# Lower attention rates beside the two later input projections of a streaming-encoder step

## The chip, the cores and the metric

One core of a Trainium2 chip runs the whole step as one program. The metric is the device time of one execution in microseconds (us). TensorE (PE) multiplies matrices, VectorE (DVE), ScalarE (ACT) and GpSimd (POOL) do the element-wise work, SyncE (SP) issues all of this kernel's DMA transfers. PE's instructions run in the order in which the program writes them; the order on the other engines is set by the framework.

## The reference

One layer of a hybrid encoder for 32 sample frames and 2048 prompt frames of width 1024, all float32:

```
u = rmsnorm(x) @ w_in                      # q, k, v (8 heads x 64) and 512 pooling channels
z = q.k / 8, for keys before the query only
a = sigmoid(z) * product of (1 - sigmoid(z)) over the keys between    # stick-breaking, no softmax
att = rmsnorm(a @ v);  pool = rmsnorm(multi-scale causal pooling of u's last 512 channels)
x = x + [att, pool] @ w_out                # output projection
x = x + (silu(h @ w_gate) * (h @ w_up)) @ w_down,  h = rmsnorm(x)     # d_ff 2816
x = x + (p @ w_ple) * sigmoid(rmsnorm(x) @ w_ple_gate);  y = rmsnorm(x)
```

The sample frames also see 256 cached keys. The new k, v and pooling rows are outputs too.

## The kernel before, in words

Every large product is done with three matmuls (`mm3`, lines 206 to 208) on operands split into a high and a low part. The 2080 frames go through two kinds of dense stages. Three **projection stages** (`project`, called P0, P1, P2 here) each take two column blocks of `WB` (288 and 384, 384 and 384, 384 and 256 frames) and store q, k, v to DRAM scratch. Then three **later stages** (`rest`, called R0, R1, R2 here) each take two column blocks of `OB` (336 and 336, then 352 each) through output projection, FFN and gated embedding.

**Attention** (`all_units`, `attn_units`, `attention`) is cut into query groups 0 to 6: group 0 is the sample frames, group 1 has 2 query tiles of 128, groups 2 to 5 have 3, group 6 has 2. For each of 8 heads a group has one unit per key segment: its own ("diagonal") segment first, then the earlier groups' segments. A unit with m query tiles and n key tiles has a cost of m*n, a diagonal one m(m+1)/2, one of group 0 a cost of 4 (`TS_COST`). It is handed out in max(m, n) **steps**, each of which writes, in PE's order, one scores product `z` (line 711), for an earlier unit the two `av` products (753, 754), and the transposes `tp` (740) that `av` needs two steps later. Behind `z` come two sigmoids on ACT (714, 715), for diagonal tiles a POOL mask (719), a scan and a product on DVE (729, 730), and behind the transposes the split of `aa` (175 on ACT, 176 on DVE). `z` and `av` have one PSUM bank each. The loads of the next unit's `q`, `kt`, `vt` are issued at the first step of the unit before it. After groups 0 and 1 the pipeline is drained with steps of cost 1. After the last unit of a group come its norm (`norm0` to `norm3`): by `LAGE` the last of it, `norm3`, which stores the group's columns of HX and sets `astate["done"]`, stands about ten steps behind the last unit, so inside the next group for groups 2 and up.

**Who runs when** is set by `drive` (lines 844 to 859): the dense generator yields costs (6 x columns / 2400 for every two of a gemm's k chunks); each is multiplied by the stage's entry in `RATES` and added to a credit, and attention steps are run until the credit is used up. P0 has rate 0; P1 and P2 have `RATES[0]` and `RATES[1]`; R0, R1, R2 have the other three. A group may not start before its q and k exist: groups 0 to 2 in P1, 3 and 4 in P2, 5 and 6 in R0.

```
            att["credit"] += cost * rate
            while att["gen"] is not None and att["credit"] > 0 and att["next"][0] <= ready:
                att["credit"] -= att["next"][1]
                step()
```

**What a later stage needs** stands in `rest` ahead of its first product (line 936): with `NEED = (2, 4, 6)` it runs steps, with nothing between them, until the norm of group 2 (R0), 4 (R1) or 6 (R2) has been written out. Only then come `load_mix`, which loads the attention and pooling columns (`as<-hx`), and, for R0, a yield of 8.0 (`BUBBLE`) ahead of the first output projection.

```
        while att["gen"] is not None and astate["done"] < NEED[OS.index(sup)]:
            step()
```

Of the kernel before, what the change touches and what calls it, by code (L numbers as in the profile page):

```python
# [55 lines left out]
LAGE = (1, 3, 6, 6, 6, 6, 6)  # L56
PREP_LEAD, PREP_COST = 3, 0.5
ACT_SLOTS, X_SLOTS = 26, 20
RATES = (1.1, 1.2, 0.9, 0.9, 0.9)


def MANUAL(nc):
# [16 lines left out]
def stickbreak_step(  # L79
# [764 lines left out]
    def drive(dense, rate, ready):  # L844
        att["ready"] = ready
        for cost in dense:
# [4 lines that stand above are left out]
            if att["credit"] > 0:  # L851
                att["credit"] = 0.0
            bg_n[0] += 1
            if bg and bg_n[0] % BG_EVERY == 0:
                try:
                    next(bg[0])
                except StopIteration:
                    bg.popleft()
# [332 lines left out]
    with tc.manual_schedule(engines=MANUAL(nc)):  # L1191
        with tc.tile_pool(name="proj", bufs=1) as pool, tc.tile_pool(name="projx", bufs=1) as xpool:
            opened = {0: open_block_pair(WS[0], xpool, pool)}

            def following(i):
                if i < len(WS):
                    opened[i] = open_block_pair(WS[i], xpool, pool)
                return opened.get(i)

            for i, sup in enumerate(WS):  # L1200
                drive(project(sup, pool, opened[i], lambda: following(i + 1)), RATES[i - 1] if i else 0.0, i - 1)
        phase["rest"] = True
        with tc.tile_pool(name="rest", bufs=1, reuse_waits="tile") as apool,                 tc.tile_pool(name="restx", bufs=1, reuse_waits="tile") as pool:
            for i, sup in enumerate(OS):
                drive(rest(sup, pool, apool), RATES[2 + i], 2)

# [31 lines left out]
```

## Time and profile before

| | |
|---|---|
| median of 3 runs | 2902.8 us (2901.12 to 2907.18) |
| profiled execution | 2903.48 us |
| its span, first to last instruction | 2901.8 us |
| PE / DVE / ACT / POOL busy | 2828.5 / 2026.4 / 1302.4 / 632.0 us |
| granted PE clock, mean | 0.992 of full speed |
| attention's first and last `z` | 176.5 and 2049.5 us |
| DMA moved | 366.50 MB, mean 126 GB/s |

A matmul's recorded duration overlaps the next one's, so a busy PE is not the measure: a stream of 384-column matmuls has starts about 0.17 us apart while each lasts 0.34 us. What counts is where PE has nothing to start.

### The profile page before, as it was taken

To read this page: it belongs to the slowest core of one execution; us is meant where nothing else is said; L and a number is where in the kernel's file an instruction comes from. 1 tells how busy PE (TensorE), PEld (TensorE's weight loads), DVE (VectorE), ACT (ScalarE), POOL (GpSimd) and SP (SyncE) were. 2 spreads that over 40 slices of the span, in tenths; PEclk is the share of its full clock that TensorE was granted. 3 is DMA by queue.
4 is the path that set the end of the run, shared out by engine and by line. 5 is a ranking of instruction groups with operands and counts; after the bars stand their busy time and mean duration, and the time that the engine had idled before them with its cause. 6 is when DMAs were issued, how large, how long until landed. Compare 5 with 4: busy or idle time off the path is not lost.

```text
span 2901.8 us, 50173 instructions
## 1 busy us (share of the span) xinstructions
PE 2828.5 (97%) x18478; PEld 2783.1 (96%) x18478; DVE 2026.4 (70%) x3498; ACT 1302.4 (45%) x2829; POOL 632.0 (22%) x1175
## 2 busy tenths in 40 slices
PE   7999889999999999999999999999999999999998
PEld 7989789999999999999999999999999999999998
DVE  6466699887878787887888777777555644444466
ACT  4454566655444445455554444444343422222243
POOL 2012223223322222232331221112132210111120
PEclk9999999999999999999999999999999999999999
DMA  6775766783333333323653333333225522222223
GB/s 192 207 226 163 196 192 199 215 257 108 102 114 94 95 92 96 113 88 104 195 175 87 93 118 109 97 102 100 80 80 170 165 73 66 72 67 68 71 86 124
DMA packets 521919, 366.50 MB, mean 126 GB/s; under 512 B 62653, under 2 KB 508925, under 8 KB 521674
## 3 DMA queue, kind: packets, MB, share of 16 engines
q1 hardware_dynamic: 521674, 363.30, 42.3%
q8 instruction: 146, 2.39, 0.3%
q14 instruction: 99, 0.81, 0.1%
HBM read 292.89 MB, written 70.32 MB: 125 GB/s over the span
## 4 chain that ended last, share of the span: by engine, by line
PE 77%; DVE 10%; issue 5%; DMA 3%; ACT 3%; POOL 1%; SPq 0%; DVEq 0%; POOLq 0%; ACTq 0%
PE mm L206 22%; PE mm L207 21%; PE mm L208 21%; PE z L711 4%; PE tp L740 3%; DVE keep L729 2%; PE av L754 2%; PE av L753 2%; DVE wlo L191 2%; DVE as L900 1%; DVE beta L730 1%; DVE aa L176 1%; DVE win L417 1%; ACT whi L190 1%; ACT as L899 1%
## 5 line engine op out<-in xcount | busy, mean ns | idle before, releaser
L206 PE MATMUL mm<-as,whi 128*128 128x352 f32 (+1 forms) x3936 | 1300.3, 330 | 1.6 <-DMA as<-hx 1.6
L207 PE MATMUL mm<-as,whi 128*128 128x352 f32 (+1 forms) x3936 | 1264.8, 321 | 0.0
L208 PE MATMUL mm<-as,wlo 128*128 128x352 f32 (+1 forms) x3936 | 1260.0, 320 | 0.0
L206 PEld LDWEIGHTS mm<-as,whi 128*128 128x128 f32 x3936 | 741.4, 188 | 3.9 <-DMA as<-hx 2.9
L207 PEld LDWEIGHTS mm<-as,whi 128*128 128x128 f32 x3936 | 741.5, 188 | 0.3 <-DVE as L900 0.3
L208 PEld LDWEIGHTS mm<-as,wlo 128*128 128x128 f32 x3936 | 741.6, 188 | 0.0
L190 ACT CAST whi<-wraw 128x1024 fp32r<-128x1024 f32 x326 | 342.5, 1051 | 480.7 <-PE mm L207 457.3
L191 DVE TENSOR_TENSOR wlo<-wraw,whi 128x1024 fp32r<-128x1024 f32 x323 | 395.6, 1225 | 78.1 <-ACT whi L190 77.0
L729 DVE TENSOR_TENSOR_SCAN keep<-keep,keep,zeros 128x384 f32<-128x384 f32 (+2 forms) x328 | 316.6, 965 | 112.0 <-ACT keep L714 111.2
L714 ACT ACTIVATE keep<-z 128x384 f32<-128x384 f32 (+3 forms) x464 | 195.8, 422 | 363.7 <-PE z L711 313.7
L984 POOL TENSOR_TENSOR sg<-sg,t 128x352 f32<-128x352 f32 (+1 forms) x132 | 158.1, 1197 | 729.0 <-ACT sg L959 718.1
L730 DVE TENSOR_TENSOR beta<-beta,keep 128x384 f32<-128x384 f32 (+3 forms) x464 | 236.9, 511 | 31.0 <-POOL beta L719 0.8
L726 POOL COPY keep<-keep 128x1 f32<-128x1 f32 (+1 forms) x328 | 147.9, 451 | 439.7 <-DVE keep L729 438.0
L711 PE MATMUL z<-kt,q 128*128 128x384 f32 (+4 forms) x928 | 212.0, 309 | 17.2 <-ACT beta L715 10.2
L176 DVE TENSOR_TENSOR aa<-tp,aa 128x384 fp32r<-128x384 f32 (+4 forms) x472 | 213.1, 451 | 16.5 <-ACT aa L175 15.7
L175 ACT CAST aa<-tp 128x384 fp32r<-128x384 f32 (+4 forms) x472 | 193.1, 409 | 66.8 <-PE tp L740 60.5
L957 DVE TENSOR_TENSOR t<-mm,rbc 128x352 f32<-128x352 f32 (+1 forms) x180 | 92.8, 515 | 162.9 <-PE mm L208 157.6
L1005 DVE TENSOR_TENSOR xs<-xs,mm 128x352 f32<-128x352 f32 (+1 forms) x288 | 144.2, 509 | 86.2 <-PE mm L208 85.6
L206 PE MATMUL mm<-hh,whi 128*128 128x384 f32 (+2 forms) x576 | 200.0, 347 | 3.8 <-ACT acc L447 2.5
L740 PE MATMUL tp<-ident,beta 128*128 128x128 f32 (+1 forms) x1112 | 199.8, 274 | 0.4 <-ACT xt L331 0.2
L715 ACT ACTIVATE beta<-z 128x384 f32<-128x384 f32 (+3 forms) x464 | 194.4, 419 | 0.0
L208 PE MATMUL mm<-hh,wlo 128*128 128x384 f32 (+2 forms) x576 | 187.4, 325 | 1.0 <-DVE wlo L191 1.0
(155 smaller groups left out, 3748.2 us busy)
## 6 DMA issues: line engine op xcount, KB each, us to landing
wraw<-in_w_ffn_gate_dram SPq DMA_DIRECT2D x66, 512.0 KB, 3.9
wraw<-in_w_ffn_up_dram SPq DMA_DIRECT2D x66, 512.0 KB, 3.9
wraw<-in_w_ffn_down_dram SPq DMA_DIRECT2D x66, 512.0 KB, 3.4
wraw<-in_w_in_dram SPq DMA_DIRECT2D x48, 512.0 KB, 5.0
wraw<-in_w_out_dram SPq DMA_DIRECT2D x48, 512.0 KB, 5.4
kt<-ks SPq DMA_DIRECT2D x112, 192.0 KB, 2.4
vt<-vs SPq DMA_DIRECT2D x112, 192.0 KB, 2.7
wraw<-in_w_ple_gate_dram SPq DMA_DIRECT2D x32, 512.0 KB, 3.9
```

The lines of the kernel that those rows point to most:

```text
L176: V.tensor_sub(lo, src, hi.bitcast(F32))
L190: S.copy(hi, raw)
L191: eng.tensor_sub(lo, raw, hi.bitcast(F32))
L206: T.matmul(ps, a[0], b[0], start=first, stop=False)
L207: T.matmul(ps, a[0], b[1], start=False, stop=False)
L208: T.matmul(ps, a[1], b[0], start=False, stop=last)
L711: T.matmul(z[:qw, :wi], hd["q"][:, e, qsl], un["k"][:, :wi], start=(e == 0), stop=(e == 1))
L714: S.activation(keep[:qw, :wi], z[:qw, :wi], AF.Sigmoid, scale=-0.125)
L715: S.activation(beta[:qw, :wi], z[:qw, :wi], AF.Sigmoid, scale=0.125)
L729: V.tensor_tensor_scan(rev, rev, zeros[:qw].broadcast_to([qw, wi]), initial=init, op0=ALU.mult, op1=ALU.add)
L730: V.tensor_mul(beta[:qw, :wi], beta[:qw, :wi], keep[:qw, 1:wi + 1])
L740: T.transpose(bank[:kw, qo[i]:qo[i] + qws[i]], un["b"][i][:qws[i], k0:k0 + kw], ident[:qws[i], :qws[i]])
```

## The change

Two numbers of one constant: the rates of P1 and P2 go from 1.1 and 1.2 to 0.75 each. The rates of R0 to R2, `NEED` and everything else stay. No instruction is added or taken away; attention steps stand at other places in PE's order, and with them their work on the other engines and their loads.

```diff
-RATES = (1.1, 1.2, 0.9, 0.9, 0.9)
+RATES = (0.75, 0.75, 0.9, 0.9, 0.9)
```

## Rows read from the trace of the kernel before

**Rows 1.** The page: PE's busy time and its share of the span in 40 slices.

```profile
PE 2828.5 (97%) x18478; PEld 2783.1 (96%) x18478; DVE 2026.4 (70%) x3498; ACT 1302.4 (45%) x2829; POOL 632.0 (22%) x1175
...
PE   7999889999999999999999999999999999999998
```

**Rows 2.** Busy time by stretch: P1 (161 to 355), P2 (355 to 573.5), R0 after its start, and the part of R1 that has attention. Columns: stretch, its length, busy time and instructions of PE, PEld, DVE, ACT, POOL, granted PE clock, DMA share, GB/s.

```profile
161.00:355.00 194.00, 176.84 (x1155) 166.23 (x1153) 124.19 (x280) 100.07 (x270) 40.21 (x119) 0.98 0.65 189
355.00:573.50 218.50, 206.77 (x1458) 199.86 (x1458) 194.48 (x374) 139.79 (x354) 68.37 (x163) 0.99 0.69 201
...
587.40:1416.00 828.60, 819.27 (x5416) 808.28 (x5415) 668.77 (x1107) 414.87 (x919) 223.68 (x415) 0.99 0.40 116
1416.00:2066.00 650.00, 647.31 (x4257) 642.11 (x4256) 514.90 (x874) 310.81 (x698) 143.80 (x270) 1.00 0.38 113
```

**Rows 3.** Waits of PE in P1 and P2 (160 to 573.5): who waited, for whom, us in total, times, longest.

```profile
PE z L711 <- DMA kt<-ks: 6.8, 4, 3.6
PE av L753 <- DVE attT L652: 5.0, 6, 1.8
PE tp L325 <- ACT xt L331: 3.4, 3, 1.4
PE z L711 <- ACT beta L715: 3.3, 5, 1.8
PE tp L325 <- DVE xt L333: 3.0, 4, 1.1
PE mm L206 <- ACT acc L447: 2.5, 2, 1.9
PE av L753 <- ACT aa L175: 0.8, 1, 0.8
```

**Rows 4.** Timeline of PE: the column sums of the norm (`norm1`) of group 1, at the end of P1, and of group 2, in P2, and the broadcast (`norm2`) of group 2.

```profile
345.86 0.61 PE L247 MATMUL tp<-ones,aacc 128*128 128x1 f32 x4 [0.16 <-POOL aacc L663]
...
522.26 0.73 PE L247 MATMUL tp<-ones,aacc 128*128 128x1 f32 x6
...
532.05 0.83 PE L268 MATMUL tp<-ident,r 128*128 128x128 f32 x6
```

**Rows 5.** Timeline of PE at the start of R0, where four attention steps stand with no dense product between them (`BUBBLE`): the first product of each step, then the first output projection.

```profile
573.51 0.52 PE L711 MATMUL z<-kt,q 128*128 128x384 f32 x2
...
575.46 0.50 PE L711 MATMUL z<-kt,q 128*128 128x256 f32 x2 [1.22 <-ACT beta L715]
...
577.05 0.51 PE L711 MATMUL z<-kt,q 128*128 128x256 f32 x2 [0.62 <-ACT beta L715]
...
578.55 0.78 PE L711 MATMUL z<-kt,q 128*128 128x256 f32 x2
...
581.23 0.65 PE L206 MATMUL mm<-as,whi 128*128 128x336 f32 x1 [0.77 <-DMA as<-hx]
...
585.48 0.56 PE L206 MATMUL mm<-as,whi 128*128 128x336 f32 x1
```

**Rows 6.** Busy time by stretch around the same place; columns as in rows 2.

```profile
573.50:577.00 3.50, 1.71 (x11) 1.14 (x9) 3.47 (x7) 3.04 (x8) 0.00 (x0) 1.00 0.87 254
577.00:580.40 3.40, 3.34 (x14) 2.73 (x14) 3.40 (x9) 1.95 (x6) 0.73 (x4) 0.58 0.83 262
580.40:587.40 7.00, 5.40 (x17) 4.32 (x17) 2.10 (x5) 0.92 (x3) 0.19 (x2) 0.50 1.06 371
```

**Rows 7.** Timeline of PE in P2: one attention step between dense products, and the dense products behind it.

```profile
558.00 0.33 PE L711 MATMUL z<-kt,q 128*128 128x128 f32 x2
...
558.82 0.43 PE L206 MATMUL mm<-hh,whi 128*128 128x384 f32 x1
559.08 0.34 PE L207 MATMUL mm<-hl,whi 128*128 128x384 f32 x1
559.26 0.34 PE L208 MATMUL mm<-hh,wlo 128*128 128x384 f32 x1
```

**Rows 8.** Groups of DVE instructions from 400 to 573.5, shapes apart: line, engine, operation, tiles, shape, count, then busy us, mean ns of one, then idle time before them.

```profile
L729 DVE TENSOR_TENSOR_SCAN keep<-keep,keep,zeros 128x256 f32<-128x256 f32 x23 | 17.1, 743 | 2.7 <-ACT keep L714 2.7
L176 DVE TENSOR_TENSOR aa<-tp,aa 128x384 fp32r<-128x384 f32 x30 | 16.2, 542 | 0.0
L730 DVE TENSOR_TENSOR beta<-beta,keep 128x256 f32<-128x256 f32 x32 | 14.2, 443 | 1.4
L729 DVE TENSOR_TENSOR_SCAN keep<-keep,keep,zeros 128x384 f32<-128x384 f32 x8 | 8.8, 1103 | 1.0 <-ACT keep L714 1.0
...
L730 DVE TENSOR_TENSOR beta<-beta,keep 128x384 f32<-128x384 f32 x15 | 8.3, 551 | 0.7
...
L652 DVE TENSOR_TENSOR attT<-av,bot 64x384 f32<-64x384 f32 x9 | 4.9, 546 | 0.2
```

**Rows 9.** Timeline of SP at the end of group 2's norm in P2: the issues of the four HX stores (`norm3`).

```profile
536.81 4.00 SPq L95 DMA_DIRECT2D hx<-aa  x3
...
542.77 0.36 SPq L95 DMA_DIRECT2D hx<-aa  x1
```

**Rows 10.** The view of DMA issues: such a store, and a load of R0's columns: engine, operation, count, KB each, median us from issue to landing.

```profile
hx<-aa SPq DMA_DIRECT2D x16, 384.0 KB, 2.7
...
as<-hx SPq DMA_DIRECT2D x16, 336.0 KB, 6.9
```

**Rows 11.** Waits of PE from 587.4 to 2235 (R0 after its start, and R1), the longest.

```profile
PE z L711 <- ACT beta L715: 5.0, 5, 1.5
```

## Prediction

> **What bounds the kernel now.** I read the page first: PE is busy nearly everywhere, and its thin slices are the first seven and a little behind, so whatever a schedule can save lies before about 600 us [rows 1]. Then the stretches: PE lacks 17.2 us of 194.0 in P1 and 11.7 us of 218.5 in P2, while R0 behind its start lacks 9 of 829 and R1 with attention 3 of 650, though both carry attention too [rows 2]. DVE is at 89% in P2 and about 80% in R0 and R1. The granted clock of 0.98 and 0.99 in P1 and P2 stands for some 4 and 2 us more. So at most 17.2 + 11.7 + 6 = 35 us can be had in the two stages that the change thins. Third, whom PE waits for there: for the loads of keys 6.8, for the `av` bank until the head is read out 5.0, for the sigmoids in the single `z` bank 3.3, for the split of `aa` 0.8, together 15.9 us that belong to attention; for x's transposes and for the pooling 3.4 + 3.0 + 2.5 us, which belong to the dense work [rows 3]. In R0 and R1 the longest sort of wait that attention causes is 5.0 us in all [rows 11]. So a step of attention is cheaper beside the later stages, and the direction of the change has a reason in the trace.
>
> **The credit account.** Which steps go where follows from the code alone. Dense costs: P1 yields 16 x 0.5 for the two columns with preparation, 3 x 7.68 for the other pooling columns, 12 x 2.56 for v, 8 x 7.68 for k and q, 123.2; P2 likewise 8 + 3 x 6.4 + 10 x 2.56 + 8 x 6.4 = 104.0. Before, that buys 1.1 x 123.2 + 1.2 x 104.0 = 260 credits. R0 wants group 2's norm written: group 0 costs 16 units x 4 + 11 of drain = 75, group 1 8 x 3 + 11 = 35, group 2 8 x (6 + 6) = 96, and `norm3` stands 11 steps (25 credits: a diagonal unit 6, one on group 2 of 9, one on group 1 of 6, two thirds of a diagonal one 4) into group 3. That is 231, so 260 are enough and the loop of line 936 has nothing to do. The trace agrees: group 2's norm is in P2 at 522 to 532 us, and group 1's at the end of P1 [rows 4].
>
> After, the two stages buy 0.75 x 227.2 = 170, with the overshoot of the last step 172. **The rates fall below what the first output projection needs**: 231 - 172 = 59 credits, which are 28 steps (17 of group 2, 11 of group 3), are run by line 936 with no dense product between them. Behind R0's start all goes as before: R0 buys 0.9 x 574 = 517 and reaches 748, over the some 640 that R1 needs; all of attention (group 3 168, 4 240, 5 312, 6 248, then 12 of drain) costs 1186, which R1 passes with 0.9 x 593 more, before its last down projection and its embedding. So R2 waits for nothing, and the end of attention moves from 2050 to some 2100 us into dense work that hides it. Of the 104 score steps of P1 and P2, 63 stay, 28 go to the bare stretch, 13 net to R0 and R1. As PE's work they cost the same there.
>
> **Part 1, gain in P1 and P2.** 41 fewer steps of 104. The waits on keys come where group 1's short units (two steps) leave too little time for the next loads; with 2.0 instead of 1.36 of dense cost for each step that time grows by half. I take 70% of attention's 15.9 us, 11; a quarter of the dense waits' 9, 2, as ACT and DVE carry less; 1.5 for the restart of some 18 matmul streams; and 2 of the 6 us of clock. Gain 16.5 us. Bounds: 8 (half of attention's waits, nothing else) and 28 (80% of the ceiling of 35).
>
> **Part 2, the bare stretch.** The trace has a small one: the four steps of `BUBBLE` at the start of R0. Their scores start at 573.51, 575.46, 577.05 and 578.55, the last step ends about 580.4: 1.95, 1.59, 1.50 and 1.85 us, mean 1.72 [rows 5]. DVE is busy for 3.47 of 3.50 and 3.40 of 3.40 us there [rows 6], so it is the bound. A check from durations [rows 8]: a step on group 1's keys gives DVE a scan of 743, a product of 443 and two thirds of a split of 542 ns, 1.55 us; a diagonal step of the same mean width some 1.65; one on group 2's keys 1103 + 551 + 542, 2.2. With 12, 13 and 3 of them, and 4 heads read out at 546 ns, DVE needs 18.6 + 21.5 + 6.6 + 2.2 = 49 us, and 28 x 1.72 is 48. I take 48.5. Between dense products the same step takes from PE 0.82 us (558.00 to 558.82), and the next product starts its follower 0.26 instead of 0.18 us later [rows 7]: 0.9, for 28 steps 25 us, and this is saved where the steps stood. Cost 48.5 - 25 = 23.5 us. Bounds: 28 x 1.50 - 25 = 17, and 28 x 1.95 - 25 = 29.5, with 1.7 us for each of four heads whose loads come late as the longest such waits do, 37.
>
> In this bare stretch the granted clock falls: it is 1.00 up to 577, 0.58 to 580.4 and 0.50 to 587.4, that is 1.2 GHz, after PE had waited between steps [rows 6]. The mean of 1.72 us holds steps on either side of the fall. The Trainium skill, "TensorE: Matmul & The Clock Gate", section "HAM oscillation — how this bites in real kernels", says that a PE that waits between short bursts is put back to half its clock and starts the next burst cold. The trace agrees at this place; what that would do to a stretch of 28 steps is the third rival.
>
> **Part 3, the projection's inputs come late.** Before, group 2's norm was written 30 us ahead of R0, and the first product waited only for the loads: from 573.5 to 585.48, when it runs on [rows 5], 12.0 us hold four steps (3.6) and four k chunks of three matmuls (1.8), so 6.6 us are lost, with the half clock about 7.5. After, `norm2` and `norm3` are issued in the last of the 28 steps, and `load_mix` must wait for the stores. In P2 the broadcast was at 532.05 [rows 4] and the four stores were issued from 536.81 to 542.77 [rows 9]; a store lands after 2.7 us, a load after 6.9 [rows 10]; the 6.9 is of loads issued all together, here they come one by one, so 5 is my estimate. So the first chunk is there 4.8 + 2.7 + 5 = 12.5 us after the broadcast, and the last attention chunk 10.7 + 2.7 + 5 = 18, by the full 6.9 20. `BUBBLE`'s four steps cover 7. Lost: 18 + 1 of slow clock - 3.6 - 1.8 = 14. Cost 14 - 7.5 = 6.5 us. Bounds 2 (stores issued as soon as the vectors allow, DVE being free) and 12. Queued behind the waiting loads on SP are the next units' `kt` and `vt`; the unit already loaded covers the bubble.
>
> **Sum**, against the profiled execution's 2903.5 us (span 2901.8, which lies 0.7 above the median of the three): 2903.5 - 16.5 + 23.5 + 6.5 = **2917 us**, 0.5% slower. The 0.7 us to the median are left aside.
>
> **The rivals.** (1) *Faster:* the thinning removes nearly all that is lost in P1 and P2, 28 to 35 us, because DVE's backlog there feeds on itself, while the bare steps keep to the fastest pace of 1.50 us and the norm hides: 2903.5 - 32 + 17 + 2 = 2890. It decides from a gain of 30 us on, over twice what PE waits for attention [rows 3]. If the account were wrong and group 2's norm were done before R0, there would be no bare stretch and 2903.5 - 16.5 = 2887; against this stands that the same account puts the norms of before where the trace has them [rows 4]. (2) *No change:* a middling gain against the lower bounds, 2903.5 - 17 + 17 + 2 = 2905.5. (3) *Much slower, by the clock:* the stretch stays at half clock; PE's part of a step doubles from 0.9 to 1.8 us and takes turns with DVE's 1.75 through the one `z` bank, which holds each score until two sigmoids have read it, so that a step takes 2.2 us: 28 x 2.2 - 25 = 36.5; with the late inputs at 12 and a gain of 13, 2903.5 - 13 + 36.5 + 12 = 2939. The skill's rule named above speaks for it. For it in the trace: 0.50 of the clock at the end of the bubble; against it: at 0.58 two steps still took 1.50 and 1.85 us [rows 5, 6].
>
> **How the numbers follow.** Slower as summed, 2909 to 2930: 0.58. Much slower by the clock, about 2939: 0.12. No change, within 0.2% (5.8 us, about what a measurement of this kernel can tell from none): 0.15. Faster: 0.15, of which 0.05 for no bare stretch at all. The likeliest case gives 2917. With the bounds the sum runs from 2903.5 - 28 + 17 + 2 = 2894.5 to 2903.5 - 8 + 37 + 12 = 2944.5; the range of 8 in 10 is 2896 to 2938. Faster 0.15, same 0.15, slower 0.70.
>
> **What the changed profile would show.** Right: P1 and P2 together about 53 us shorter (41 steps at 0.9 and 16.5 of waits); `z<-kt` waits mostly gone; group 2's column sums behind the last projection product; then some 48 us with `z`, `tp` and `av` alone on PE, DVE near 100%, the clock at half; then waits on `as<-hx` longer than before. Wrong would be group 2's norm before the last q columns, bare steps clearly off 1.7 us, P1 and P2 still holding their waits, or a bare stretch ahead of R1 or R2.

## The result and the profile after

The changed kernel takes 2932.11 us (median of 4 runs, 2930.87 to 2934.8) against 2901.96 us before in the same comparison: ratio 1.0103, 95% interval 1.0091 to 1.0115. It is slower by some 30 us; forecast were 13.5. The profiled execution took 2931.66 us, its span is 2929.9 us, 28.1 longer than before.

The page of the kernel after, PE's busy time and its share in 40 slices, to be read beside [rows 1]:

```profile
PE 2842.3 (97%) x18478; PEld 2791.8 (95%) x18478; DVE 2036.5 (70%) x3498; ACT 1305.8 (45%) x2829; POOL 633.4 (22%) x1175
...
PE   7999989899999999999999999999999999999998
```

The digits hardly show it: two slices of 8 in either page, one of them three places further on. PE's busy time has even grown by 14 us, with the same 18478 instructions, since a matmul at half clock is busy for longer (the mean granted clock is 0.987 in place of 0.992). The stretches say more. Kernel after, by stretch (columns as in [rows 2]): P1 and P2, the 28 bare steps, R0's start with the bubble, then R0 from its first output product on, and R1.

```profile
162.60:530.30 367.70, 344.71 (x2335) 330.42 (x2334) 254.10 (x518) 192.92 (x489) 74.45 (x199) 0.99 0.65 194
...
530.30:579.40 49.10, 38.28 (x183) 29.76 (x183) 45.97 (x93) 33.40 (x93) 23.59 (x63) 0.83 0.73 210
579.40:599.60 20.20, 11.80 (x44) 9.12 (x43) 10.67 (x19) 6.21 (x14) 3.70 (x5) 0.66 0.84 277
...
590.00:1426.50 836.50, 822.65 (x5415) 811.75 (x5414) 668.54 (x1110) 416.18 (x923) 224.41 (x416) 0.99 0.38 112
1426.50:2253.20 826.70, 820.65 (x5348) 814.25 (x5347) 624.97 (x1054) 386.46 (x848) 189.73 (x326) 1.00 0.37 111
```

And the same stretches of the kernel before, cut at the same instructions (the last product of P0, of P2, the first and last of R0, the last of R1):

```profile
164.10:573.40 409.30, 380.41 (x2589) 362.90 (x2588) 316.65 (x649) 238.96 (x621) 108.59 (x282) 0.99 0.67 196
581.20:1414.50 833.30, 823.11 (x5422) 811.11 (x5423) 668.57 (x1109) 414.69 (x919) 223.77 (x415) 0.99 0.40 117
1414.50:2225.10 810.60, 806.47 (x5262) 800.88 (x5261) 600.28 (x1017) 371.96 (x811) 181.41 (x308) 1.00 0.37 111
```

DVE is busy for 45.97 of the bare stretch's 49.10 us, PE's clock there is 0.83. PE's idle time in P1 and P2 has fallen only from 28.9 to 23.0 us, and R1, where by the account nothing but twelve more steps was expected, is 16.1 us longer.

PE's timeline after, at the ends of the bare stretch: its first two scores, group 2's column sums and broadcast, the first score of `BUBBLE`, and the start of the output projection.

```profile
530.35 0.33 PE L711 MATMUL z<-kt,q 128*128 128x128 f32 x2
...
531.88 0.50 PE L711 MATMUL z<-kt,q 128*128 128x256 f32 x2 [0.67 <-ACT beta L715]
...
572.17 1.44 PE L247 MATMUL tp<-ones,aacc 128*128 128x1 f32 x6 [0.33 <-POOL aacc L663]
...
578.57 1.08 PE L268 MATMUL tp<-ident,r 128*128 128x128 f32 x6
579.40 0.60 PE L711 MATMUL z<-kt,q 128*128 128x384 f32 x2
...
587.25 0.69 PE L753 MATMUL av<-aa,vt 128*128 128x384 f32 x1 [3.74 <-ACT aa L175]
...
590.04 0.63 PE L206 MATMUL mm<-as,whi 128*128 128x336 f32 x1
...
593.52 0.65 PE L206 MATMUL mm<-as,whi 128*128 128x336 f32 x1 [2.29 <-DMA as<-hx]
```

The column sums stand at 572, not at 522 as in [rows 4]. Between the last projection product and the first output product 64 scores are recorded, two to a step: 32 steps, the 28 of the account and the four of `BUBBLE`. From 530.35 to 579.40 the 28 take 49.05 us. The next rows answer to [rows 5]: the bubble's `av` waits 3.74 us for `aa`, whose buffers the norm shares, then the second chunk of the product waits 2.29 us for its load.

PE's waits after, in P1 and P2 (columns as in [rows 3]):

```profile
PE tp L325 <- DVE xt L333: 3.1, 3, 1.7
PE tp L325 <- ACT xt L331: 2.3, 4, 1.3
PE av L753 <- DVE attT L652: 2.3, 3, 0.9
PE mm L208 <- DVE wlo L191: 2.1, 2, 1.5
PE mm L206 <- ACT uu L175: 1.8, 2, 1.5
PE mm L207 <- DVE uu L176: 1.6, 2, 0.9
PE z L711 <- ACT beta L715: 1.6, 2, 1.2
PE z L711 <- DMA kt<-ks: 1.5, 1, 1.5
PE tp L268 <- issue: 1.5, 1, 1.5
PE mm L206 <- DVE up L412: 1.2, 1, 1.2
PE mm L206 <- ACT acc L447: 1.1, 2, 0.6
PE mm L206 <- ACT whi L190: 0.9, 1, 0.9
```

Attention's waits are down from 15.9 us [rows 3] to 5.4 (2.3 + 1.6 + 1.5). In their place stand waits of the dense work on its own operands, 7.6 us (2.1 + 1.8 + 1.6 + 1.2 + 0.9): the splits of weights (`wlo`, `whi`) and of the pooling operands (`uu`), the pooling input `up`. Before, they were 1.8 us, with no wait for `uu`; from the same view as [rows 3]:

```profile
PE mm L206 <- DVE up L412: 0.8, 1, 0.8
PE mm L208 <- DVE wlo L191: 0.6, 1, 0.6
...
PE mm L206 <- ACT whi L190: 0.4, 1, 0.4
```

### The profile page after: what moved, and what is told of

Read it like the earlier page. It is cut to its first block, busy times and chain, and to the rows that moved or that the text cites. A ratio compares the mean times of both kernels' runs of the same rounds, so it can differ in the third digit from the quotient of the medians.

```text
span 2929.9 us, 50208 instructions
## 1 busy us (share of the span) xinstructions
PE 2842.3 (97%) x18478; PEld 2791.8 (95%) x18478; DVE 2036.5 (70%) x3498; ACT 1305.8 (45%) x2829; POOL 633.4 (22%) x1175
## 3 DMA queue, kind: packets, MB, share of 16 engines
q1 hardware_dynamic: 521674, 363.30, 41.6%
## 4 chain that ended last, share of the span: by engine, by line
PE 80%; DVE 8%; issue 5%; ACT 3%; DMA 2%; POOL 1%; SPq 0%; DVEq 0%; POOLq 0%; ACTq 0%
PE mm L206 23%; PE mm L207 22%; PE mm L208 22%; PE z L711 4%; PE tp L740 4%; PE av L754 2%; PE av L753 2%; DVE keep L729 1%; DVE wlo L191 1%; DVE as L900 1%; DVE win L417 1%; DVE beta L730 1%; ACT whi L190 1%; PE tp L268 1%; DMA wraw<-in_w_in_dram 1%
```

## Experiments

Three theories. **A:** the loss is the bare stretch and the inputs that come late behind it. **D:** what PE loses in P1 and P2 is largely the dense work's own, and thinning attention only uncovers it. **B**, formed after the first four runs: the kernel before is at a favourable placement of its steps that other rates lose, whether anything runs bare or not. For each run the table has the median and, of its profiled execution, the length of P1 and P2, the time from there to the first output product, R0 and R1 (cut as above), with the score steps that the account puts into each. From R1's last product to the end of the span it is 676.7 to 677.1 us everywhere. The unchanged kernel's median in the comparisons of the single runs is 2902.7 to 2904.7. A stage's length is that of one profiled execution; where the order on PE was the same, P1 and P2 differ by up to 6.8 us (365.9 in e5, 372.7 in e1), so a few microseconds of one stage show nothing by themselves.

| run | median us | steps P1+P2 / bare / R0 / R1 | P1+P2 | to first product | R0 | R1 |
|---|---|---|---|---|---|---|
| before | 2902.0 | 104 / 0 / 208 / 152 | 409.3 | 7.8 | 833.2 | 810.6 |
| after | 2932.1 | 63 / 28 / 209 / 164 | 367.7 | 59.8 | 836.5 | 826.7 |
| e1_no_group2 | 2918.5 | 63 / 0 / 213 / 188 | 372.7 | 9.0 | 840.5 | 854.4 |
| e2_rates_zero | 2998.8 | 0 / 121 / 209 / 164 | 306.1 | 184.1 | 841.5 | 824.0 |
| e3_just_enough | 2919.3 | 94 / 0 / 209 / 161 | 406.9 | 10.3 | 836.5 | 826.5 |
| e4_more_z_banks | 2932.3 | 63 / 28 / 209 / 164 | 368.3 | 58.9 | 833.5 | 828.4 |
| e5_pool_first | 2926.9 | 63 / 28 / 209 / 164 | 365.9 | 59.8 | 831.4 | 826.8 |
| e6_rates_09 | 2921.3 | 80 / 11 / 209 / 164 | 383.1 | 35.1 | 838.9 | 824.2 |
| e7_just_enough_pool_first | 2919.6 | 94 / 0 / 209 / 161 | 403.3 | 10.6 | 835.4 | 824.3 |
| e8_rates_up | 2918.7 | 113 / 0 / 206 / 145 | 429.5 | 9.4 | 832.4 | 808.1 |
| e9_p2_slightly_up | 2924.5 | 106 / 0 / 208 / 150 | 416.5 | 8.0 | 841.1 | 816.9 |
| e10_r0_up | 2914.1 | 104 / 0 / 218 / 142 | 412.2 | 8.0 | 852.8 | 803.6 |
| e11_p2_alone | 2921.1 | 84 / 7 / 209 / 164 | 389.6 | 27.7 | 836.6 | 825.6 |
| e12_before_pool_first | 2902.6 | 104 / 0 / 208 / 152 | 408.5 | 7.8 | 834.2 | 810.7 |

(Of e2's 121 bare steps 30 have no score.)

**The bare stretch taken away.**

```diff
-NEED = (2, 4, 6)
+NEED = (1, 4, 6)
-                dma(p, HX[:, c, :, C0[b]:C0[b] + N[b]].rearrange("a p n -> p a n"))
+                dma(p, HX[:, c + 4 if b < 2 and c < 4 else c, :, C0[b]:C0[b] + N[b]].rearrange("a p n -> p a n"))
```

> The changed kernel, but R0 asks only for group 1's norm before it starts, and its output projection reads the pooling half of HX twice in place of the attention half (so attention's part is left out of R0's output projection; all of attention is still computed). By the credit account no step is then run bare; the 28 steps go between R0's and R1's dense products. Theory A (the loss is the bare stretch and the late inputs): 49 - 25 = 24 us and some 8 us come back, 2932 -> 2900 (2895 to 2905). Rival (attention is dearer beside the later stages than beside the projections): the time stays above 2920, and R0 and R1 are longer by more than 0.9 to 1.1 us for each step moved.

2918.48 us (ratio to before 1.0049, 1.0035 to 1.0063, before being at 2904.7 in this comparison): of the 30 us, 13.6 come back and not 32. The stretch ahead of R0 shrinks from 59.8 to 9.0 us, but R0 takes 4.0 and R1 27.7 us more for the 28 steps, 31.7 / 28 = 1.13 us a step. P1 and P2, whose order on PE is unchanged, are 5.0 longer. So A is right that the bare stretch costs, but the steps are not had for 0.9 us beside the later stages, and some 14 us of loss against the kernel before are left where nothing runs bare. Both the number of A and that of its rival are missed.

**No attention in P1 and P2.**

```diff
-RATES = (0.75, 0.75, 0.9, 0.9, 0.9)
+RATES = (0.0, 0.0, 0.9, 0.9, 0.9)
```

> Both rates 0: no attention in P1 and P2, 121 bare steps ahead of R0. Theory A prices each bare step at 1.75 us against 0.9 between dense products: 2902 + 121 x 0.85 + 7 - what P1 and P2 gain, some 3000. The second question is what P1 and P2 lose without any attention: if their waits are the dense work's own (theory D), PE's idle time there stays at 15 to 23 us (28.9 before, 23.0 after the change); if they are attention's (my prediction), it falls below 10.

2998.8 us in one run. This run's stretch from P0 to the last product of P2, and PE's longest waits in it:

```profile
164.70:470.80 306.10, 289.75 (x1976) 283.74 (x1976) 173.45 (x296) 132.67 (x264) 27.30 (x50) 1.00 0.61 186
```

```profile
PE mm L206 <- ACT acc L447: 3.4, 2, 2.8
PE tp L325 <- ACT xt L331: 3.0, 1, 3.0
PE tp L325 <- DVE xt L333: 2.8, 3, 1.5
PE mm L206 <- ACT v L531: 2.8, 1, 2.8
PE mm L207 <- DVE uu L176: 1.7, 2, 1.0
```

With no attention at all PE still idles for 306.10 - 289.75 = 16.4 us, and each of these waits is for the dense work's own values: D. From here a step in P1 and P2 costs (367.7 - 306.1) / 63 = 0.98 us up to the changed kernel's 63 and (409.3 - 306.1) / 104 = 0.99 us up to the 104 of before, waits included. Their price doesn't rise with their density; in R1 it is (854.4 - 826.7) / 24 = 1.15 us from the kernel after to e1.

That difference is one of the steps' size and not of the place. Counting from the shapes in the traces the columns that attention's products and transposes (`z`, `av`, `tp`) stream through PE, P1 and P2 have 114,048 before and 56,704 after: 57,344 fewer in the 41 steps, for 41.6 us, 0.73 us for 1000 columns. R1 has 22,016 more after than before for 16.1 us, 0.73 again, and 37,760 more in e1 than in the kernel after for 27.7 us, 0.73 once more. A step taken out of P1 and P2 has 1400 columns in the mean, one added to R1 1690. So thinning P1 and P2 moves work to where it is no cheaper.

**Just enough attention.**

```diff
-RATES = (0.75, 0.75, 0.9, 0.9, 0.9)
+RATES = (1.05, 1.05, 0.9, 0.9, 0.9)
```

> Both rates 1.05: by the account the lowest equal rates at which group 2's norm is still inside P2 (in its last q columns), no bare step; 9 steps fewer in P1 and P2 than before. Theory A with D: within 0.2% of before, 2896 to 2904. If the thinning itself were worth what I predicted (16.5 us for 41 steps), 9 steps would give 3 to 4 us, 2898; if the norm's latency alone is dear, some 5 us more than before, 2907.

2919.25 us (1.0055, 1.0041 to 1.0068), above all that was expected. Nothing runs bare but three bubble steps; group 2's column sums are at 546.8 us, in P2. R1 has 15.9 us more for nine steps, the first output product waits 3.9 us for `as<-hx`, and P1 and P2 are only 2.4 us shorter for ten steps fewer. This run is what called for theory B.

**More banks for the scores.**

```diff
-                    z = ps_z.tile([128, 512], F32, tag="z", name=nm("z"))
+                    z = mm_bank() if phase.get("bare") else ps_z.tile([128, 512], F32, tag="z", name=nm("z"))
...
+        phase["bare"] = True
         while att["gen"] is not None and astate["done"] < NEED[OS.index(sup)]:
             step()
+        phase["bare"] = False
```

> The changed kernel with the scores of the bare stretch written to the idle banks of the dense products in turn, in place of the one z bank. If DVE sets the pace of the bare stretch (its busy time there is 46.0 of 49.1 us): the stretch stays at 46 to 49 us and the time within 4 us of 2932. If the single z bank and the two sigmoids that empty it set the pace: 1.3 to 1.5 us a step, the stretch 37 to 42 us, the time 2920 to 2925.

2932.27 us. This run's bare stretch:

```profile
532.40:580.00 47.60, 35.54 (x179) 30.80 (x179) 45.16 (x92) 32.18 (x93) 23.71 (x63) 0.79 0.74 210
```

DVE is busy for 45.16 of 47.60 us. The longest waits of PE in the stretch of the changed kernel, 8.4 us in 13 times, name the sigmoids that empty the one `z` bank; with four banks in turn in its place the stretch is 1.5 us shorter and the time the same. DVE sets the pace, and the wait named is where PE stands when DVE is behind.

**The pooling half first.**

```diff
+KORD = (4, 5, 6, 7, 0, 1, 2, 3)
...
-            for c in range(KC):
+            for c in KORD:
                 p = slot(b)
...
-                yield from gemm(ps, [(kpart(wu, k), mix[b][k]) for k in range(KC)])
+                yield from gemm(ps, [(kpart(wu, k), mix[b][j]) for j, k in enumerate(KORD)])
```

> The changed kernel, but R0 to R2 load the pooling half of HX ahead of the attention half and multiply by it first, so that the four chunks that wait for group 2's norm come last in each product. Theory A (some 8 us of the loss are the inputs that come late behind the bare stretch): the first product starts while the norm is stored, 2932 -> 2923 to 2928. Rival (the start of R0 is bound by the loads' number or by PE's half clock): within 3 us of 2932.

2926.94 us (1.0081, 1.0065 to 1.0098): 5 us back. The first product is no earlier, 590.29 us, as the bubble's steps stand ahead of it. Timeline of PE in this run (lines are one higher, by the added constant):

```profile
590.29 0.63 PE L207 MATMUL mm<-as,whi 128*128 128x336 f32 x1
590.72 0.48 PE L208 MATMUL mm<-as,whi 128*128 128x336 f32 x1
...
592.12 0.48 PE L207 MATMUL mm<-as,whi 128*128 128x336 f32 x1
592.40 0.37 PE L208 MATMUL mm<-as,whi 128*128 128x336 f32 x1
592.61 0.31 PE L209 MATMUL mm<-as,wlo 128*128 128x336 f32 x1
592.77 0.32 PE L207 MATMUL mm<-as,whi 128*128 128x336 f32 x1
```

It runs on, and the starts are 0.15 us apart from 592.4 on instead of 0.28; in the changed kernel the second chunk waits 2.3 us and the slow pace lasts to 599.5. So here a wait at the start cost its length and then the slow clock behind it. Theory A had the number, but not the path: the first product did not start earlier.

**Fewer bare steps.**

```diff
-RATES = (0.75, 0.75, 0.9, 0.9, 0.9)
+RATES = (0.9, 0.9, 0.9, 0.9, 0.9)
```

> Both rates 0.9: by the account 11 bare steps in place of 28. Theory A: each bare step costs 0.85 us over its place between dense products, so 17 fewer give 14 us back: 2918. If the loss hung on the norm's lateness alone and not on the number of bare steps: the same time as with 28 steps, 2932, and as with none (rates 1.05 gave 2919 with the norm inside P2, but late).

2921.31 us (1.006, 1.0043 to 1.0078): 17 bare steps fewer give 10.8 us, 0.64 each, where A had 14 us. The scores recorded ahead of the first output product are 30, the 11 + 4 steps of the account.

**Just enough, and the pooling half first**: e3 with the edit of e5.

> Rates 1.05 with the pooling half first. At 1.05 there is no bare step, yet the time was 2919 and not 2902. If the late norm is the larger part of those 17 us (PE idle 7.1 us ahead of the first output product and 3.6 us more in R0 than before): 2908 to 2913. If it is the changed alignment in P1, P2 and R1 (PE idle 5.7 and 2.7 us more there, clock loss 3.4 and 3.4): within 3 us of 2919.

2919.62 us (1.0055, 1.004 to 1.0071), the same as e3. But the edit did not take the wait away. PE's wait for the loads in this run (lines one higher), and the last stores of group 2's norm and the first loads of R0's columns on SP in e3:

```profile
PE mm L207 <- DMA as<-hx: 4.0, 1, 4.0
...
560.67 6.35 SPq L95 DMA_DIRECT2D hx<-aa  x4
...
576.72 7.97 SPq L95 DMA_DIRECT2D as<-hx  x12
```

The first output product waits 4.0 us for its loads, as it did in e3 (3.9), though its first chunks no longer hang on the norm. In e3 the stores are issued by 567.0 us and the loads from 9.7 us later on. So it is not the norm that these loads wait for; what their lateness costs, this run doesn't show.

**The other way.**

```diff
-RATES = (0.75, 0.75, 0.9, 0.9, 0.9)
+RATES = (1.2, 1.3, 0.9, 0.9, 0.9)
```

> The other way: rates 1.2 and 1.3, 9 score steps more in P1 and P2 than before, 7 fewer in R1, no bare step, group 2's norm earlier. If attention's waits in P1 and P2 made thinning worth anything, this is slower than before by 3 to 5 us. If a step costs PE the same everywhere and the dense work's own waits are what P1 and P2 lose, it is within 0.2% of before, 2898 to 2908.

2918.68 us (1.0053, 1.0036 to 1.007): more attention beside the projections loses as much as less of it, and far more than either expectation has.

**Near the kernel before.** Three edits of that kernel: P2's rate, R0's rate, and half of the change.

```diff
-RATES = (1.1, 1.2, 0.9, 0.9, 0.9)
+RATES = (1.1, 1.25, 0.9, 0.9, 0.9)
```

> The kernel before with P2's rate at 1.25 in place of 1.2: by the account two steps move from R1 to P2, P1 is the same, nothing runs bare. All other rates tried, up and down, stand at 2918 to 2921 where no or few steps are bare, and only 2 of those us are explained by each step's place. Theory B (the kernel before stands at a favourable alignment in P1, P2 and R1, worth some 10 to 16 us, that any other rate loses): 2908 to 2919. Theory A alone (what counts is the bare stretch and the late norm): within 0.2% of before, 2899 to 2907.

2924.54 us (1.0072, 1.0055 to 1.0089), beyond what even B expected: two steps that change their stage, and with them another place for every step behind P2's start, cost 20.6 us. By stretch, P1 and P2, R0 and R1 of this run:

```profile
163.10:579.60 416.50, 382.23 (x2598) 365.19 (x2597) 320.82 (x655) 241.75 (x627) 108.50 (x283) 0.98 0.66 192
587.50:1428.60 841.10, 825.59 (x5414) 814.77 (x5415) 667.29 (x1107) 415.47 (x918) 221.66 (x411) 0.99 0.39 116
1428.60:2245.50 816.90, 808.02 (x5256) 801.54 (x5255) 599.38 (x1012) 370.67 (x806) 182.94 (x306) 1.00 0.37 110
```

All three are longer than before, by 7.2, 7.8 and 6.3 us, with PE idle for 34.3, 15.5 and 8.9 us in place of 28.9, 10.2 and 4.1: 15.5 of the 21.3 us are idle time.

```diff
-RATES = (1.1, 1.2, 0.9, 0.9, 0.9)
+RATES = (1.1, 1.2, 0.95, 0.9, 0.9)
```

> The kernel before with R0's rate at 0.95 in place of 0.9; P1 and P2 keep their order, 10 steps move from R1 to R0. If a step costs PE the same in R0 and R1 and nothing hangs on alignment there: within 0.2% of before. Theory B with the part that lies in R1 (3 to 6 us in every other rate tried): 2905 to 2910, P1 and P2 unchanged at 409 us.

2914.11 us (1.0038, 1.0025 to 1.0051). Ten steps from R1 to R0 lengthen R0 by 19.6 us and shorten R1 by 7.0; for the 15,104 columns moved that is 1.30 us for 1000 in R0 and 0.46 in R1, so next to the kernel before the even price of 0.73 does not hold. The order in P1 and P2 is that of before, and they are 2.9 us longer. B, but more in R0 than expected.

```diff
-RATES = (1.1, 1.2, 0.9, 0.9, 0.9)
+RATES = (1.1, 0.75, 0.9, 0.9, 0.9)
```

> Half of the change: P1 keeps 1.1, P2 has 0.75. By the account 7 bare steps. Theory A from the runs with 11 and 28 bare steps (2921 and 2932, 0.6 us a step): 2919. If the loss were the late norm alone, the same as with 28, 2932; if the number of bare steps alone against before, 7 x 0.85: 2909.

2921.06 us (1.0059, 1.0044 to 1.0074). 20 scores are recorded ahead of the first output product, the 7 + 3 steps of the account. The time is near A's 2919, which was read off e6 and the kernel after; the 2909 that seven bare steps alone would give against the kernel before is missed by 12.

**Before, with the pooling half first**: the kernel before with the edit of e5.

> The kernel before with the pooling half of HX first, as in the run that gained 5 us on the changed kernel. Before, the first output product waits only 1.6 us for the loads and group 2's norm is long done: expected within 0.2% of before, at best 2 us faster; theory B would have it slower, as the order of loads in R0 changes too.

2902.59 us; ratio 0.9995, 0.9986 to 1.0004: no change. The order of R0's first loads and chunks alone loses nothing, against B's guess for it; what the other runs changed is the place of attention's steps. No run beat the kernel before.

## Why the prediction was right in direction and too small

By its own steps, against the differences of the two traces (P0 is 1.5 us shorter, by itself; from the bubble's first score to R0's last product it is 1414.46 - 573.51 before and 1426.52 - 579.40 after):

| term | forecast us | measured us |
|---|---|---|
| P1 and P2: 41 steps of 0.9 out, and 16.5 of gain | -53.4 | -41.6 |
| the 28 bare steps | +48.5 | +49.05 |
| from the bubble to R0's end (inputs late) | +6.5 | +6.2 |
| R1, 13 steps of 0.9 | +11.7 | +16.1 |

**The credit account** held to the step: 32 bare steps with the bubble, R2 waiting for nothing. **Part 2** was right in pace and in reason: 48.5 / 28 = 1.73 us a step forecast from DVE's durations and the bubble, 49.05 / 28 = 1.75 measured, and e4 showed DVE and not the bank behind it. (Its upper bound adds up to 29.5 + 4 x 1.7 = 36.3 and not 37.) **Part 3** was right in size (6.2), and e5 gave back 5 us when the product didn't wait. Its path was right in part: the bubble, which was to cover 7 us, took 10.6 (579.40 to 590.04), since its own `av` products waited 3.7 and 1.1 us for `aa`; the wait for the loads behind it was 2.3.

**The step that failed is "Gain 16.5 us"** in part 1, and under it the sentence that a step is cheaper beside the later stages. Of 53.4 us that P1 and P2 were to lose they lost 41.6: beside the 36.9 for 41 steps of 0.9 that is a gain of 4.7. Attention's waits fell as forecast, by 10.5 of 15.9 us; but they were not lost time that could be had back. PE's idle time fell by 5.9 us, as waits for weights and pooling operands that weren't split yet rose from 1.8 to 7.6 us; the granted clock in the two stages stayed at a mean of 0.99. That PE came to these products too early, because attention no longer held it back, is the likely reading and not shown by a run. e2 showed the ceiling: with no attention at all 16.4 of the 28.9 us of idle time stay, so 12.5 us is all that the thinning of every step gave, and a step's price is 0.98 to 0.99 us however densely they stand.

The miss of 4.4 us in R1 is a matter of size. The one step in P2 that 0.9 was read off [rows 7] has 1408 columns, 0.64 us for 1000; the 22,016 columns added to R1 come to 14.1 us by that, and to the 16.1 measured by the 0.73 that the 41 steps cost in P1 and P2, waits included. So a column moved from there to R1 was neither dearer nor cheaper, and moving it gained nothing.

With that, the sum without its gain is 2903.5 + 23.5 + 6.5 = 2933.5, against 2931.66 profiled. By stage it comes out the same. Every moved column is priced at 0.73 us for 1000, which leaves no loss in P1 and P2 by the choice of the price, and none in R1 by measurement. Ahead of the first output product 38,912 more columns would cost 28.4 us, and the stretch grew by 59.8 - 7.8 = 52.0: 23.6 are lost. R0 has 3,584 columns fewer, which should save 2.6 us, and is 3.3 longer: 5.9 are lost. The same count gives 18 us for e11 with 7 bare steps and 23 for e6 with 11, so a good part of this loss doesn't grow with the number of bare steps.

**What the prediction didn't have at all:** the kernel before stands at a placement from which every shift tried loses, also where nothing runs bare: two steps 20.6 us (e9), ten from R1 to R0 10 us (e10), nine or ten either way 15 to 16 (e3, e8), each against the runs of before beside it. By totals the 30 us would then divide into some 14 for the bare stretch and its late inputs (2932.1 against 2918.5 without them, e1) and some 14 to 16 that the other rates tried cost as well. The two accounts disagree over e1: it wins 50.8 us ahead of R0, and its 38,656 more columns in R0 and R1 would cost 28.2 at 0.73, but they cost 31.7, and its P1 and P2 are 5.0 longer in an unchanged order. Whether the kernel after pays for its placement, or e1 pays for another one, no run decides.

Of the rivals, none happened as written. *Faster* needed a gain of 30 us; PE's idle time in the two stages fell by 5.9. *No change* needed the lower bounds of both costs; they came near their middle. *Much slower, by the clock*, forecast 2939, which is near in time, but by a pace of 2.2 us that didn't come: the clock fell to a mean of 0.83 in the bare stretch, yet with DVE busy for 94% of it the steps kept to 1.75 us; only behind the stretch, at 0.66 up to 599.6, did the clock cost. The Trainium skill, "TensorE: Matmul & The Clock Gate", section "HAM oscillation — how this bites in real kernels", says that waits between short bursts put PE back to half its clock; the trace agrees with the fall. The measured 2932 lies just above the 2909 to 2930 of the likeliest case and within the range, which was wide enough for a gain that didn't come.

**Open:** why the placement before is favourable. The loss of e9 is spread over P1 and P2, R0 and R1, in single waits of up to 3.6 us on different engines; no one wait was found that accounts for it, and no run held the order of one engine and changed another's.

## What to carry to other kernels

When a schedule hands out filler work by credits, add up the credits up to each point where the rest is forced: rates that fall 59 credits short show in the account as 28 steps with nothing beside them, each at the pace of its slowest engine. Waits that name the filler are not a gain to be booked; ask what PE would wait for next if the filler weren't there, best by a run without it. Fillers differ in size, so price them by the columns they stream and not by the step. And a schedule in which the shift of two steps costs 0.7% has to be judged against its neighbours as well as against its own best point.

## What the runs showed that was not expected

Two of 464 score steps, some 2 us of PE's work, moved between stages that had PE at 93% (P1 and P2) and 99% (R1) busy, with the steps between them shifted, changed the time by 20.6 us, and did so in each of four runs (2923.66 to 2926.52). A wait of 2.3 us at R0's start, hidden in e5, was worth 5 us, since PE went on at half clock behind it: starts 0.28 us apart up to 599.5 us instead of 0.15 from 592.4 on.
